# The gather pipeline of a mixture-of-experts layer given out in another order, with 92 instead of 96 gathered tokens

## Chip, cores and metric

The kernel runs on one core of a Trainium2 chip. The metric is the device time of one launch in microseconds (us); the time before is the median of three runs. "Profile" and "trace" mean one execution recorded by the hardware profiler. PE is the matrix engine (TensorE), DVE is VectorE, ACT is ScalarE, POOL is GpSimd and SP is the sync engine, which here only issues loads.

## The reference, cut to what matters

Two blocks run over 256 tokens of width 2048. The first (gated convolution and attention) and the front of the second (convolution and a state-space branch) are not touched by the change. What matters is the last layer, a product-key expert layer with 16384 experts of one neuron each, in float32:

```python
s = einsum('thcd,hcnd->thcn', (xb @ w_q), sub_keys)   # 8 heads, 2 halves, 128 keys
s_top, i_top = top_k(s, 16)
cand = s_top[:, :, 0, :, None] + s_top[:, :, 1, None, :]
best, pos = top_k(cand, 16)                            # 16 experts a head, 128 a token
gates = softmax(best)
act = gelu(einsum('td,thkd->thk', xb, u_tab[expert]))
y = einsum('thk,thkd->td', gates * act, v_tab[expert])
x = x + y;  return rmsnorm(x, norm_final)
```

## The kernel before

The first 1226 us of the trace are dense layers. Then the 256 tokens of the expert layer are split by token and computed in two ways at the same time.

**Dense, for the last NT = 160 tokens.** All 16384 experts are computed, 128 at a time. A *u step* multiplies one 1 MB tile of `u` with the normed tokens (16 matrix products, recorded as 32 matmuls of 160 columns, since each float32 product takes two) and ACT writes gelu of the result (`u_step`). A *v step* multiplies one 1 MB tile of `v` with the weighed activations and adds into PSUM (`v_step`). There are 128 of each: 60 u steps first, then v and u alternating (68 pairs), then 60 v steps. The last `LAST` v steps are done bank by bank, so that one bank is finished while the next is multiplied. Tiles come through a ring of `NR = 5` buffers on SP's queue; the load of tile n+5 goes out when step n has used its buffer. PE writes u results to two PSUM banks in turn, so it can be at most two u steps ahead of ACT.

The weights of the dense part are the gates spread into a 128x128 table for each token. `gbuild` makes them from one-hot rows: four tokens at a time, DVE and ACT write the rows, PE multiplies them (8 matmuls), ACT copies the result out, and every 16 tokens a DMA writes the table `gd` to memory. `gload` reads a block of it back for 8 experts' rows, and DVE's `weigh` multiplies the activations with it ahead of each v step.

**Gathered, for the first NS_ = 96 tokens.** `sparse` fetches only the 128 chosen rows of a token: in each of 3 groups of 32 tokens, one gather brings 128 rows of 8 KB (32 tokens x 4 experts), 1 MB, into one of 5 buffers. An *item* is one gather and one DVE instruction of 2.3 us on it: a product and sum with the token (u item) or a scaled add (v item). The 192 items come as four u items, then four v items of the block of u items before. After four u items ACT takes gelu of their 4 columns. The gather of item m+5 is issued on POOL right behind item m, whose buffer it needs. At the end the four partial sums of a token go through memory (`sd`) and are added on DVE, normed and written out.

**The order.** There is no scheduler: instructions stand on each engine in the order in which the Python code runs. After each step, `Weave.run(budget)` lets generators (`topk`, `sparse`) emit as much as a budget of estimated ns allows; a `yield None` ends a generator's turn until the next step. `run_fine` does the same for `gbuild`, four times in a step. Each engine works through its own list, so an instruction that waits holds up all behind it on that engine. `hand_out` puts expert indices and gates of the first 128 tokens into the layout that the gathers read (`rbuf`).

Of the kernel before, what the change touches and what calls it, by code (L numbers as in the profile page):

```python
# [107 lines left out]
def body(ctx, tc, xT, par, wst, kst, bblk, cblk, gfin, uexp, vexp, out):  # L108
# [1090 lines left out]
    flat = lambda ap: ap.rearrange("p h k -> p (h k)")  # L1199
    sp_ready = [False]  # L1200

    def hand_out():


        V = nc.vector
        V.scalar_tensor_tensor(out=flat(ab[:, 0]), in0=flat(idx[:, 0]), scalar=float(P), in1=flat(idx[:, 1]),
                               op0=ALU.mult, op1=ALU.add)
        V.tensor_copy(flat(abu[:, 0]), flat(ab[:, 0]))
        V.tensor_copy(abr[:, P:2 * P], flat(gat))
        both = abr.rearrange("p (c s) -> p c s", c=2)  # L1210
        for g in range(SG):
            for q in range(4):
                nc.gpsimd.dma_start(
                    rbuf[32 * q:32 * q + 32, 64 * g:64 * g + 64].rearrange("p (c s) -> p c s", c=2),
                    both[32 * g:32 * g + 32, :, 32 * q:32 * q + 32])
        sp_ready[0] = True

    def topk():
        V = nc.vector
        for tt in range(2):  # L1220
            for h in range(NH + 1):
# [29 lines left out]
            yield 2500
            o4 = scor[tt].rearrange("p (h a b) -> p h a b", h=8, a=16)
            for c in range(2):
                for h in range(0, NH, 4):
                    for q in range(4):
                        V.tensor_tensor(out=o4[:, h + q], in0=ab[:, c, h + q, :, None].to_broadcast([P, 16, 16]),
                                        in1=iota[:, None, 0:16].to_broadcast([P, 16, 16]), op=ALU.is_equal)
                    for q in range(4):
                        V.tensor_tensor(out=o4[:, h + q], in0=o4[:, h + q],
                                        in1=ixf[:, h + q, c, None, :].to_broadcast([P, 16, 16]), op=ALU.mult)  # L1260
                    V.tensor_reduce(out=idx[:, c, h:h + 4, :], in_=o4[:, h:h + 4], axis=AX.X, op=ALU.add)
                    yield 3900
# [15 lines left out]
    GB = [B[6], B[7]]  # L1278
    oh = [[S[22][:, (8 * n + k) * P:(8 * n + k + 1) * P] for k in range(8)] for n in range(2)]
    pend_g = []  # L1280

    def gbuild():
        for t4 in range(NT // 4):
            sg = stg[(t4 // 4) % 2].rearrange("p (i t) -> p t i", t=16)
            pb = GB[t4 % 2]
            t = NS_ + t4 * 4
            nc.vector.tensor_tensor(
                out=S[22][:, (t % 8) * P:(t % 8 + 4) * P].rearrange("p (t j) -> p t j", t=4),
                in0=iota[:, None, :].to_broadcast([P, 4, P]),
                in1=i2T[:, t:t + 4, None].to_broadcast([P, 4, P]), op=ALU.is_equal)  # L1290
            for q in range(4):
                o, tq = oh[1][(t + q) % 8], slice(t + q, t + q + 1)
                if q < 1:
                    nc.scalar.activation(o, iota, AF.Abs, scale=-1.0, bias=i1T[:, tq])
                    nc.scalar.activation(o, o, AF.Relu, scale=ngT[:, tq], bias=gT[:, tq])
                else:
                    nc.vector.tensor_scalar(o, iota, i1T[:, tq], gT[:, tq], op0=ALU.is_equal, op1=ALU.mult)
            yield 1650 - 256 * 1
            pend_g.append((t4, pb, sg))
            if len(pend_g) > 1:  # L1300
                gmm(*pend_g.pop(0))
        while pend_g:
            gmm(*pend_g.pop(0))
            yield 500

    def gmm(t4, pb, sg):
        for q in range(4):
# [4 lines left out]
        if t4 % 4 == 3:  # L1312
            nc.scalar.dma_start(gd[t4 // 4], stg[(t4 // 4) % 2].rearrange("p (i t) -> p i t", t=16))

    gblk = lambda b: stg[b % 2][:, 0:8 * NT].rearrange("p (n i t) -> p n i t", n=NT // 16, i=8)

    def gload(b):
        nc.gpsimd.dma_start(gblk(b), gd[:, :, 8 * b:8 * b + 8, :].rearrange("n p i t -> p n i t"))

    def weigh(i):  # L1320

        a3 = act_at(i).rearrange("p (n t) -> p n t", n=NT // 16)
        nc.vector.tensor_tensor(out=a3, in0=a3, in1=gblk(i // 8)[:, :, i % 8, :], op=ALU.mult)  # L1323
        if i % 8 == 7 and i // 8 + 2 < 16:
            gload(i // 8 + 2)


    acc_s, x_rep, gaddr = S[10], S[19], rbuf.bitcast(U32)
    dots = sqsum

    def sparse():
# [4 lines left out]
        flat_b = [(g, n) for g in range(SG) for n in range(8)]  # L1336
# [5 lines left out]
        items += [("v", SG - 1, 28 + k) for k in range(4)]  # L1342

        def gather(m):
            kind, g, k = items[m]
            nc.gpsimd.indirect_dma_start(  # L1346
                out=gb[m % len(gb)][:], out_offset=None, in_=uexp if kind == "u" else vexp,
                in_offset=bass.IndirectOffsetOnAxis(ap=gaddr[:, 64 * g + k:64 * g + k + 1], axis=0))

        def rows(g):  # L1350
            for q in range(4):
                nc.gpsimd.dma_start(x_rep[32 * q:32 * q + 32, :], S[18][32 * g:32 * g + 32, :])

        rows(0)
        for m in range(len(gb)):
            gather(m)
        yield None
        for m, (kind, g, k) in enumerate(items):
            buf = gb[m % len(gb)]
            d, a = dots[:, 32 * g + k:32 * g + k + 1], dots[:, P + 32 * g + k:P + 32 * g + k + 1]  # L1360
            if kind == "u":
                V.tensor_tensor_reduce(out=buf, in0=buf, in1=x_rep, scale=1.0, scalar=0.0,  # L1362
                                       op0=ALU.mult, op1=ALU.add, accum_out=d)
# [282 lines left out]
```

## Time and profile before

| what | value |
|---|---|
| median of 3 runs | 2569.36 us (2566.88 to 2573.03) |
| profiled execution, its own time | 2564.76 us |
| its span in the trace | 2563.0 us |
| PE busy | 2397.4 us, 94% |
| DVE, ACT, POOL busy | 62%, 27%, 26% |
| moved by DMA | 741.94 MB |

The span runs from the first instruction to the last. Busy time of PE is modelled, so its share is no measure of how near it is to its peak; what counts is which wait ends last in each stretch. The DMA share is that of the core's 16 DMA engines (1.01 is all of them all the time).

### The profile page before, as it was taken

The page shows a single profiled execution, that of the slowest core. Times are in us where ns is not written, and L with a number is a line of the kernel's source. Part 1 is how long each engine was busy: PE and PEld are TensorE (multiplying, and loading weights), DVE is VectorE, ACT ScalarE, POOL GpSimd, SP SyncE. Part 2 cuts the span into 40 slices and gives each one's busy share as a digit, 9 for nine tenths or more (in the row PEclk, how much of TensorE's full clock was granted, in tenths as well). Part 3 has the DMA queues.
Part 4 walks back from the last instruction along what each step waited for, and adds up shares of the span by engine and source line. Part 5 has one row for each costly group of instructions (what it writes and reads, how often), then busy time and mean ns, then how long its engine had stood idle before and what let it go on. Part 6 is the DMA issues. An engine that isn't in the chain of part 4 may idle for free.

```text
span 2563.0 us, 40064 instructions
## 1 busy us (share of the span) xinstructions
PE 2397.4 (94%) x16832; PEld 2270.2 (89%) x16832; DVE 1587.9 (62%) x2379; ACT 696.5 (27%) x1043; POOL 659.5 (26%) x853
## 2 busy tenths in 40 slices
PE   8999999999999999999879994999999899999987
PEld 7888888899999999888879994988888888999887
DVE  6767777589999977567497665344444344414433
ACT  5544454443244445453114520000000000000002
POOL 1887888300000000230202124221111221021100
PEclk9999999999999999999989997999999999999999
DMA  6455556565555444564789999999999999999994
GB/s 234 175 187 188 191 181 215 196 239 206 197 205 183 173 174 176 192 226 165 251 309 389 393 396 360 379 416 421 417 416 416 381 418 416 394 355 412 412 351 176
DMA packets 110004, 741.94 MB, mean 289 GB/s; under 512 B 12832, under 2 KB 13184, under 8 KB 24032
## 3 DMA queue, kind: packets, MB, share of 16 engines
q1 hardware_dynamic: 65760, 474.50, 49.1%
q0 software_dynamic: 36864, 241.81, 23.7%
q10 hardware_dynamic: 7200, 23.07, 2.4%
q8 instruction: 132, 2.16, 0.3%
q14 instruction: 48, 0.39, 0.0%
HBM read 707.00 MB, written 29.10 MB: 287 GB/s over the span
## 4 chain that ended last, share of the span: by engine, by line
PE 63%; DMA 27%; DVE 5%; issue 2%; ACT 1%; POOL 1%; SPq 0%; POOLq 0%; DVEq 0%; ACTq 0%
DMA s<-in_vexp_dram 14%; PE b L270 13%; PE b L1475 10%; PE b L1458 10%; DMA s<-in_wst_dram 9%; PE b L271 7%; PE b L255 4%; PE b L257 4%; PE b L256 4%; PE b L400 2%; DVE s L173 2%; PE b L248 2%; PE b L247 2%; PE b L246 2%; DMA s<-in_uexp_dram,rbuf 2%
## 5 line engine op out<-in xcount | busy, mean ns | idle before, releaser
L1458 PE MATMUL b<-s,s 128*128 128x160 f32 x4096 | 584.9, 302 | 61.3 <-ACT s L1461 38.5
L1475 PE MATMUL b<-s,s 128*128 128x160 f32 x4096 | 583.4, 302 | 54.5 <-DMA s<-in_vexp_dram 44.5
L1458 PEld LDWEIGHTS b<-s,s 128*128 128x128 f32 x4096 | 565.5, 191 | 73.3 <-ACT s L1461 39.2
L1475 PEld LDWEIGHTS b<-s,s 128*128 128x128 f32 x4096 | 563.7, 191 | 71.9 <-issue 57.6
L270 PE MATMUL b<-s,s 128*128 128x512 f32 x1680 | 597.6, 399 | 0.0
L271 PE MATMUL b<-s,s 128*128 128x256 f32 x1680 | 471.5, 281 | 9.1 <-DVE s L173 9.0
L173 DVE TENSOR_TENSOR s<-s,s 128x2048 fp32r<-128x2048 f32 x192 | 452.4, 2358 | 28.1 <-issue 12.3
L1362 DVE CUSTOM_DVE_ANT_0 s<-s,s 128x2048 f32<-128x2048 f32 x96 | 219.7, 2291 | 275.0 <-DMA s<-in_uexp_dram,rbuf 241.6
L270 PEld LDWEIGHTS b<-s,s 128*128 128x128 f32 x1680 | 315.9, 188 | 71.4
L1374 DVE SCALAR_TENSOR_TENSOR s<-s,sqsum,s 128x2048 f32<-128x2048 f32 x93 | 218.7, 2351 | 258.8 <-DMA s<-in_vexp_dram,rbuf 258.1
L167 ACT ACTIVATE s<-s 128x2048 fp32r<-128x2048 f32 x192 | 365.7, 1906 | 9.6 <-DMA s<-in_wst_dram 9.6
L271 PEld LDWEIGHTS b<-s,s 128*128 128x128 f32 x1680 | 317.7, 189 | 13.4 <-DVE s L173 12.6
L255 PE MATMUL b<-s,s 128*128 128x256 f32 x896 | 256.6, 286 | 0.0
L257 PE MATMUL b<-s,s 128*128 128x256 f32 x896 | 253.5, 283 | 0.0
L256 PE MATMUL b<-s,s 128*128 128x256 f32 x896 | 253.5, 283 | 0.0
L1461 ACT ACTIVATE s<-b 128x160 f32<-128x160 f32 x128 | 38.0, 300 | 765.3 <-PE b L1458 756.1
L1346 POOL DMA_INDIRECT s<-in_vexp_dram,rbuf x96 | 106.6, 1110 | 458.8 <-DVE sqsum L1362 196.1
L1346 POOL DMA_INDIRECT s<-in_uexp_dram,rbuf x96 | 114.3, 1191 | 382.3 <-DVE s L1323 174.7
L255 PEld LDWEIGHTS b<-s,s 128*128 128x128 f32 x896 | 171.8, 192 | 3.7 <-issue 2.9
L256 PEld LDWEIGHTS b<-s,s 128*128 128x128 f32 x896 | 171.9, 192 | 0.3
L257 PEld LDWEIGHTS b<-s,s 128*128 128x128 f32 x896 | 171.9, 192 | 0.0
L814 POOL TENSOR_TENSOR sqsum<-sqsum,s 128x256 f32<-128x256 f32 x28 | 57.9, 2067 | 385.5 <-ACT s L812 385.5
(302 smaller groups left out, 2441.8 us busy)
## 6 DMA issues: line engine op xcount, KB each, us to landing
s<-in_wst_dram SPq DMA_DIRECT2D x320, 1024.0 KB
s<-in_vexp_dram SPq DMA_DIRECT2D x128, 1024.0 KB
gd<-s ACTq DMA_DIRECT2D x10, 1024.0 KB
s<-gd POOLq DMA_DIRECT2D x16, 640.0 KB
tabd<-s POOLq DMA_DIRECT2D x32, 256.0 KB
s<-tabd ACTq DMA_DIRECT2D x32, 256.0 KB
xd<-s POOLq DMA_DIRECT2D x4, 1024.0 KB
s<-in_bblk_dram ACTq DMA_DIRECT2D x8, 512.0 KB
```

The costliest lines, as they stand in the source:

```text
L167: nc.scalar.activation(hi_of(i), raw_of(i), AF.Copy)
L173: nc.vector.tensor_tensor(out=lo_of(i), in0=raw_of(i), in1=FV(hi_of(i)), op=ALU.subtract)
L255: nc.tensor.matmul(ps, a, xh, start=(j == 0), stop=False)
L256: nc.tensor.matmul(ps, a, xl, start=False, stop=False)
L257: nc.tensor.matmul(ps, b, xh, start=False, stop=(j == len(perm) - 1))
L270: nc.tensor.matmul(ps, a, x2, start=(j == 0), stop=False)
L271: nc.tensor.matmul(ps[:, :T], b, x2[:, :T], start=False, stop=(j == len(perm) - 1))
L1346: nc.gpsimd.indirect_dma_start(out=gb[m % len(gb)][:], out_offset=None, in_=uexp if kind == "u" else vexp, in_offset=bass.IndirectOffsetOn ...
L1362: V.tensor_tensor_reduce(out=buf, in0=buf, in1=x_rep, scale=1.0, scalar=0.0, op0=ALU.mult, op1=ALU.add, accum_out=d)
L1374: V.scalar_tensor_tensor(out=acc_s, in0=buf, scalar=a, in1=acc_s, op0=ALU.mult, op1=ALU.add)
L1458: nc.tensor.matmul(ps, raw[:, k * P:(k + 1) * P], nv(k)[:, NS_:T], start=(k == 0), stop=(k == KT - 1))
L1475: nc.tensor.matmul(acc[d], raw[:, d * P:(d + 1) * P], act_at(i), start=False, stop=(i == P - 1 and (d % 3 == 2 or d == KT - 1)))
```

## The change

1. Tokens: the third group has 28 instead of 32 tokens, so 92 tokens are gathered and 164 are dense. Every dense matmul has 164 columns. The 64 gathers of the third group fetch 112 rows, not 128. `weigh` gets a second small instruction for the 4 tokens beyond 160, whose table stays on the chip (`rest`). Loads and stores of all gathered tokens (`sd`, `xrow`, `out`) have 92 rows.
2. `hand_out` is split: the indices go out before the softmax of the gates, and the index work of the first four heads (`picks`) moves up into the top-k loop.
3. `sparse` issues its first five gathers and then lets `AHEAD = 5` turns go by before the first item. The gelu of four u items is emitted two items later.
4. The first two `gload`s are issued on ACT's queue, not POOL's.
5. Budgets: while `gbuild` runs, `sparse` gets 1000 instead of 1500 for a step and `gbuild` 3400 instead of 2700. `LAST` is 2, not 4.

```diff
-SG = 3
-NS_ = 32 * SG
+GROUPS = [(0, 32), (32, 32), (64, 28)]
+NS_ = 92
...
-    def hand_out():
+    def hand_out(c):
...
+                if h == 5:
+                    yield from picks(tt, 0)
+            yield from picks(tt, 4)
+            if tt == 0:
+                hand_out(0)
             V.tensor_tensor(out=gat, in0=best, in1=best[:, :, 0:1].to_broadcast([P, 8, 16]), op=ALU.subtract)
             nc.scalar.activation(gat, gat, AF.Exp)
...
             if tt == 0:
-                hand_out()
+                hand_out(1)
...
+        if GR:
+            nc.vector.tensor_tensor(out=a[:, GT:NT], in0=a[:, GT:NT], in1=rest[:, i, :], op=ALU.mult)
...
+            if m == 0:
+                rows(0)
+        for _ in range(AHEAD):
+            yield None
+        late = []
...
                 if k % 4 == 3:
-                    lo, hi = 32 * g + k - 3, 32 * g + k + 1
-                    nc.scalar.activation(dots[:, P + lo:P + hi], dots[:, lo:hi], AF.Gelu_apprx_tanh)
+                    late.append((m + 2, acts[:, k - 3:k + 1], dots_[:, k - 3:k + 1]))
...
+            while late and m >= late[0][0]:
+                _, dst, src = late.pop(0)
+                nc.scalar.activation(dst, src, AF.Gelu_apprx_tanh)
...
-        u_step(i, 1500.0 if weave.fine else 4200.0, 2700.0 / 4)
+        u_step(i, 1000.0 if weave.fine else 4200.0, 3400.0 / 4)
...
-    gload(0)
-    gload(1)
+    gload(0, nc.scalar)
+    gload(1, nc.scalar)
...
-    LAST = 4
+    LAST = 2
```

**First place: ACT, where the first gelu of the gathered part stands.** L1461 (L1488 after) is the gelu that empties a u step's PSUM bank (`b0` or `b1`), L1366 (L1401 after) the gelu of four gathered columns in `sqsum`. Before, it stands behind the 9th u step's row:

```order
L1461 ACTIVATE s14_10958<-b1_66 128x160
L1461 ACTIVATE s14_10958<-b0_65 128x160
L1271 ACTIVATE s24_86<-b5_70 128x128 x3
L1272 ACTIVATE s24_86<-b5_70 128x128
L1366 ACTIVATE sqsum_88<-sqsum_88 128x4
L1461 ACTIVATE s14_10958<-b1_66 128x160
```

In the changed program the first one stands behind the 29th u step's row, among the copies of `gbuild` (L1323, L1307, L1308):

```order
L1326 DMA gd_10086<-s11_10074 128x2048
L1307 ACTIVATE s22_10081<-iota_10171,s24_86 128x128
L1308 ACTIVATE s22_10081<-s22_10081,s24_86 128x128
L1401 ACTIVATE sqsum_88<-sqsum_88 128x4
L1488 ACTIVATE s16_10966<-b1_66 128x164
```

It moved back by 20 u steps. Before, the first seven stand behind u steps 9, 24, 33, 45, 51, 56 and 60; after, behind 29, 38, 46, 50, 55, 59 and 64. The copies of `gbuild` stand behind u steps 28 to 47 before and 26 to 42 after.

**Second place: POOL, where the u steps end and the v steps begin.** L1346 (L1364 after) are gathers, L1318 the `gload`s, and the memset is what PE's first matmuls into the v sums need. Before:

```order
L1346 DMA s13_11202<-in_vexp_dram,rbuf_87 128x2048
L1346 DMA s5_11198<-in_vexp_dram,rbuf_87 128x2048
L1318 DMA s23_10082<-gd_10086 128x10x128
L1318 DMA s11_10074<-gd_10086 128x10x128
L1468 MEMSET s22_12892 128x512
L1346 DMA s6_11199<-in_vexp_dram,rbuf_87 128x2048
```

After, on POOL:

```order
L1364 DMA s5_11196<-in_uexp_dram,rbuf_87 128x2048
L1364 DMA s6_11197<-in_uexp_dram,rbuf_87 128x2048
L1495 MEMSET s22_12915 128x512
L1364 DMA s7_11198<-in_uexp_dram,rbuf_87 128x2048
L1364 DMA s12_11199<-in_vexp_dram,rbuf_87 128x2048
```

and on ACT, where the two loads went:

```order
L1488 ACTIVATE s8_12645<-b1_66 128x164
L1488 ACTIVATE s8_12645<-b0_65 128x164
L1401 ACTIVATE sqsum_88<-sqsum_88 128x4
L1331 DMA s23_10082<-gd_10086 128x10x128
L1331 DMA s11_10074<-gd_10086 128x10x128
L1488 ACTIVATE s8_12645<-b1_66 128x164
```

The two loads left POOL's list and stand on ACT behind the gelu of item 40. Ahead of this place 51 gathers stand on POOL before, 47 after, and 46 items on DVE before, 42 after. When `gbuild` ends, 24 items stand ahead on DVE before (47 u steps done), 11 after (42 done). Ahead of the loads of the saved tokens (L1510, L1537 after) 161 gathers stand before, 157 after; the last item stands with step 240 of 256 before, 246 after.

**Third place: PE's last steps.** L1475 (L1502 after) are v products into banks `b2` to `b7`, L1553 (L1580 after) the transposes of a finished bank; `s0` to `s4` are the tile buffers. Before, four tiles are taken bank by bank:

```order
L1475 MATMUL b3_68<-s8_12626,s2_80 128x160 x3
L1475 MATMUL b3_68<-s8_12626,s3_10964 128x160 x3
L1475 MATMUL b3_68<-s8_12626,s4_10965 128x160 x3
L1475 MATMUL b3_68<-s8_12626,s0_78 128x160 x3
L1553 MATMUL b0_65<-ident_74,s14_16747 128x128 x3
```

After, two:

```order
L1502 MATMUL b3_68<-s8_12645,s4_10971 128x164 x3
L1502 MATMUL b3_68<-s8_12645,s0_78 128x164 x3
L1580 MATMUL b0_65<-ident_74,s14_16938 128x128 x3
```

Half of the products that stood between two banks' transposes moved ahead of the first bank.

## Rows read from the trace of the kernel before

**Rows 1.** Windows: stretch, length, busy us (x records) by engine, PEclk, DMA share, GB/s.

```profile
1367.00:1491.00 124.00, 124.00 (x969) 124.00 (x968) 88.55 (x185) 73.47 (x141) 15.77 (x14) 1.00 0.99 396
1491.00:1575.00 84.00, 59.55 (x411) 58.82 (x409) 51.03 (x34) 5.89 (x17) 31.24 (x22) 0.88 1.01 416
1575.00:1597.00 22.00, 8.95 (x34) 8.27 (x35) 6.79 (x10) 0.20 (x1) 6.27 (x6) 0.52 0.71 267
1597.00:2206.00 609.00, 559.46 (x3943) 538.05 (x3943) 264.74 (x240) 19.93 (x74) 135.91 (x133) 1.00 1.01 409
2206.00:2259.00 53.00, 51.47 (x373) 50.62 (x373) 13.13 (x16) 1.61 (x6) 0.31 (x2) 1.00 0.84 330
2259.00:2344.00 85.00, 84.62 (x622) 84.21 (x621) 29.04 (x30) 0.60 (x3) 21.20 (x23) 1.00 1.01 405
2344.00:2457.00 113.00, 104.82 (x736) 100.42 (x736) 49.92 (x53) 1.90 (x4) 17.69 (x19) 1.00 1.01 412
2457.00:2531.00 74.00, 66.24 (x466) 65.14 (x467) 17.92 (x26) 4.21 (x4) 5.08 (x10) 0.98 0.93 314
```

**Rows 2.** Waits from 1220 to 1600 us: waiter, releaser, us in total, times, longest.

```profile
ACT sqsum L1366 <- DVE sqsum L1362: 95.5, 7, 27.8
...
PE b L1458 <- ACT s L1461: 38.5, 3, 20.3
```

**Rows 3.** The chain that ended last: start, length, what.

```profile
1225.84 4.36 PE b L1458 x32
...
1575.42 14.73 DMA s<-gd
...
1814.48 20.10 DMA s<-in_vexp_dram
...
2523.25 7.63 DMA s<-in_vexp_dram
```

**Rows 4.** Timeline of PE: start, length, instruction, [idle before <-releaser].

```profile
1372.45 1.05 PE L1309 MATMUL b<-s 128*128 128x128 f32 x8
1373.34 2.34 PE L1458 MATMUL b<-s,s 128*128 128x160 f32 x16
1375.52 1.05 PE L1309 MATMUL b<-s 128*128 128x128 f32 x8
```

**Rows 5.** Timeline of POOL, same columns.

```profile
1577.41 0.61 POOL L1468 MEMSET s<- 128x512 f32 x1
...
2205.21 0.95 POOL L1346 DMA_INDIRECT s<-in_vexp_dram,rbuf  x1 [4.04 <-DVE s L1323]
2258.84 0.94 POOL L1510 DMA_DIRECT2D s<-xd  x1 [52.69 <-PE b L1458]
```

**Rows 6.** Timeline of DVE, same columns.

```profile
1244.07 1.22 DVE L1261 TENSOR_REDUCE s<-s 128x64 f32<-128x1024 f32 x1
...
1248.00 1.22 DVE L1261 TENSOR_REDUCE s<-s 128x64 f32<-128x1024 f32 x1
...
1545.31 2.29 DVE L1362 CUSTOM_DVE_ANT_0 s<-s,s 128x2048 f32<-128x2048 f32 x1 [2.68 <-DMA s<-in_uexp_dram,rbuf]
...
1550.29 2.29 DVE L1362 CUSTOM_DVE_ANT_0 s<-s,s 128x2048 f32<-128x2048 f32 x1 [2.68 <-DMA s<-in_uexp_dram,rbuf]
...
2457.37 2.35 DVE L1374 SCALAR_TENSOR_TENSOR s<-s,sqsum,s 128x2048 f32<-128x2048 f32 x1 [2.50 <-DMA s<-in_vexp_dram,rbuf]
...
2483.70 2.29 DVE L1391 TENSOR_TENSOR s<-s,s 96x2048 f32<-96x2048 f32 x1 [22.57 <-DMA s<-sd]
...
2500.56 2.29 DVE L1391 TENSOR_TENSOR s<-s,s 96x2048 f32<-96x2048 f32 x1 [3.00 <-DMA s<-xrow]
...
2532.11 0.66 DVE L1546 TENSOR_TENSOR s<-b,s 128x480 f32<-128x480 f32 x1 [22.72 <-PE b L1475]
...
2549.14 0.64 DVE L1546 TENSOR_TENSOR s<-b,s 128x480 f32<-128x480 f32 x1
...
2552.10 0.30 DVE L1546 TENSOR_TENSOR s<-b,s 128x160 f32<-128x160 f32 x1
```

More of the change, by code (lines that the diff above doesn't have):

```diff
@@ L1110, in body @@
     gd = drp.tile([NT // 16, P, P, 16], F32, name="gd")
+    GT, GR = NT // 16 * 16, NT % 16
     for c in range(2):
@@ L1200, in body @@
     sp_ready = [False]
-    def hand_out():
+    def hand_out(c):
         V = nc.vector
[L1206 to L1211, printed above, removed]
-            for q in range(4):
[L1213 to L1216, printed above, removed]
+        if c == 0:
+            V.scalar_tensor_tensor(out=flat(ab[:, 0]), in0=flat(idx[:, 0]), scalar=float(P), in1=flat(idx[:, 1]),
+                                   op0=ALU.mult, op1=ALU.add)
+            V.tensor_copy(flat(abu[:, 0]), flat(ab[:, 0]))
+        else:
+            V.tensor_copy(abr[:, P:2 * P], flat(gat))
+        for g, (t0, n) in enumerate(GROUPS):
+            for q in range(4):
+                nc.gpsimd.dma_start(rbuf[n * q:n * q + n, 64 * g + 32 * c:64 * g + 32 * c + 32],
+                                    abr[t0:t0 + n, P * c + 32 * q:P * c + 32 * q + 32])
+        if c == 0:
+            sp_ready[0] = True
@@ new lines, in picks @@
+    def picks(tt, h):
+        V = nc.vector
+        hs = slice(h, h + 4)
+        V.tensor_copy(ixf[:, hs], ix[:, hs])
+        V.tensor_scalar(abu[:, 0, hs], pos[:, hs], 4, None, op0=ALU.logical_shift_right)
+        V.tensor_scalar(abu[:, 1, hs], pos[:, hs], 15, None, op0=ALU.bitwise_and)
+        V.tensor_copy(ab[:, :, hs], abu[:, :, hs])
+        yield 900
+        o4 = scor[tt].rearrange("p (h a b) -> p h a b", h=8, a=16)
+        for c in range(2):
+            for q in range(4):
+                V.tensor_tensor(out=o4[:, h + q], in0=ab[:, c, h + q, :, None].to_broadcast([P, 16, 16]),
+                                in1=iota[:, None, 0:16].to_broadcast([P, 16, 16]), op=ALU.is_equal)
+            for q in range(4):
+                V.tensor_tensor(out=o4[:, h + q], in0=o4[:, h + q],
+                                in1=ixf[:, h + q, c, None, :].to_broadcast([P, 16, 16]), op=ALU.mult)
+            V.tensor_reduce(out=idx[:, c, hs, :], in_=o4[:, hs], axis=AX.X, op=ALU.add)
+            yield 3900
@@ L1250, in topk @@
             V.tensor_tensor(out=gat, in0=gat, in1=gsum[:, 8:16, None].to_broadcast([P, 8, 16]), op=ALU.mult)
[L1251 to L1262, printed above, removed]
             if tt == 0:
-                hand_out()
+                hand_out(1)
             yield None
@@ L1280, in body @@
     pend_g = []
+    rest = S[24][:, 0:P * GR].rearrange("p (i t) -> p i t", t=GR) if GR else None
     def gbuild():
         for t4 in range(NT // 4):
-            sg = stg[(t4 // 4) % 2].rearrange("p (i t) -> p t i", t=16)
+            sg = stg[(t4 // 4) % 2].rearrange("p (i t) -> p t i", t=16) if t4 * 4 < GT else rest.rearrange("p i t -> p t i")
             pb = GB[t4 % 2]
@@ L1311, in gmm, with gload @@
                              pb.rearrange("p (t i) -> p t i", t=4), AF.Copy)
-        if t4 % 4 == 3:
+        if t4 % 4 == 3 and t4 * 4 < GT:
             nc.scalar.dma_start(gd[t4 // 4], stg[(t4 // 4) % 2].rearrange("p (i t) -> p i t", t=16))
-    gblk = lambda b: stg[b % 2][:, 0:8 * NT].rearrange("p (n i t) -> p n i t", n=NT // 16, i=8)
-    def gload(b):
-        nc.gpsimd.dma_start(gblk(b), gd[:, :, 8 * b:8 * b + 8, :].rearrange("n p i t -> p n i t"))
+    gblk = lambda b: stg[b % 2][:, 0:8 * GT].rearrange("p (n i t) -> p n i t", n=GT // 16, i=8)
+    def gload(b, eng):
+        eng.dma_start(gblk(b), gd[:, :, 8 * b:8 * b + 8, :].rearrange("n p i t -> p n i t"))
     def weigh(i):
-        a3 = act_at(i).rearrange("p (n t) -> p n t", n=NT // 16)
+        a = act_at(i)
+        a3 = a[:, 0:GT].rearrange("p (n t) -> p n t", n=GT // 16)
         nc.vector.tensor_tensor(out=a3, in0=a3, in1=gblk(i // 8)[:, :, i % 8, :], op=ALU.mult)
+        if GR:
+            nc.vector.tensor_tensor(out=a[:, GT:NT], in0=a[:, GT:NT], in1=rest[:, i, :], op=ALU.mult)
         if i % 8 == 7 and i // 8 + 2 < 16:
-            gload(i // 8 + 2)
+            gload(i // 8 + 2, nc.gpsimd)
     acc_s, x_rep, gaddr = S[10], S[19], rbuf.bitcast(U32)
+    AHEAD = 5
     dots = sqsum
@@ L1335, in sparse @@
         gb = slots([5, 6, 7, 12, 13])
-        flat_b = [(g, n) for g in range(SG) for n in range(8)]
+        flat_b = [(g, n) for g in range(len(GROUPS)) for n in range(8)]
         items = []
@@ L1341, in sparse @@
                 items += [("v", flat_b[j - 1][0], 4 * flat_b[j - 1][1] + k) for k in range(4)]
-        items += [("v", SG - 1, 28 + k) for k in range(4)]
+        items += [("v", len(GROUPS) - 1, 28 + k) for k in range(4)]
         def gather(m):
             kind, g, k = items[m]
+            n = 4 * GROUPS[g][1]
             nc.gpsimd.indirect_dma_start(
-                out=gb[m % len(gb)][:], out_offset=None, in_=uexp if kind == "u" else vexp,
-                in_offset=bass.IndirectOffsetOnAxis(ap=gaddr[:, 64 * g + k:64 * g + k + 1], axis=0))
+                out=gb[m % len(gb)][0:n, :], out_offset=None, in_=uexp if kind == "u" else vexp,
+                in_offset=bass.IndirectOffsetOnAxis(ap=gaddr[0:n, 64 * g + k:64 * g + k + 1], axis=0))
@@ L1350, in rows @@
         def rows(g):
+            t0, n = GROUPS[g]
             for q in range(4):
-                nc.gpsimd.dma_start(x_rep[32 * q:32 * q + 32, :], S[18][32 * g:32 * g + 32, :])
-        rows(0)
+                nc.gpsimd.dma_start(x_rep[n * q:n * q + n, :], S[18][t0:t0 + n, :])
         for m in range(len(gb)):
             gather(m)
-        yield None
+            if m == 0:
[3 more added lines that the diff above has]
+        late = []
         for m, (kind, g, k) in enumerate(items):
-            buf = gb[m % len(gb)]
-            d, a = dots[:, 32 * g + k:32 * g + k + 1], dots[:, P + 32 * g + k:P + 32 * g + k + 1]
+            t0, n = GROUPS[g]
+            buf = gb[m % len(gb)][0:4 * n, :]
+            dots_, acts = dots[0:4 * n, 32 * g:32 * g + 32], dots[0:4 * n, P + 32 * g:P + 32 * g + 32]
+            ac = acc_s[0:4 * n, :]
@@ L1361, in sparse @@
             if kind == "u":
-                V.tensor_tensor_reduce(out=buf, in0=buf, in1=x_rep, scale=1.0, scalar=0.0,
-                                       op0=ALU.mult, op1=ALU.add, accum_out=d)
+                V.tensor_tensor_reduce(out=buf, in0=buf, in1=x_rep[0:4 * n, :], scale=1.0, scalar=0.0,
+                                       op0=ALU.mult, op1=ALU.add, accum_out=dots_[:, k:k + 1])
                 if k % 4 == 3:
-                    lo, hi = 32 * g + k - 3, 32 * g + k + 1
-                    nc.scalar.activation(dots[:, P + lo:P + hi], dots[:, lo:hi], AF.Gelu_apprx_tanh)
+                    late.append((m + 2, acts[:, k - 3:k + 1], dots_[:, k - 3:k + 1]))
@@ L1367, in sparse @@
             else:
+                a = acts[:, k:k + 1]
                 if k % 4 == 0:
-                    a4 = dots[:, P + 32 * g + k:P + 32 * g + k + 4]
-                    V.tensor_tensor(out=a4, in0=a4, in1=rbuf[:, 64 * g + 32 + k:64 * g + 36 + k], op=ALU.mult)
+                    a4 = acts[:, k:k + 4]
+                    V.tensor_tensor(out=a4, in0=a4, in1=rbuf[0:4 * n, 64 * g + 32 + k:64 * g + 36 + k], op=ALU.mult)
                 if k == 0:
-                    V.tensor_scalar(acc_s, buf, a, None, op0=ALU.mult)
+                    V.tensor_scalar(ac, buf, a, None, op0=ALU.mult)
@@ L1373, in sparse @@
                 else:
-                    V.scalar_tensor_tensor(out=acc_s, in0=buf, scalar=a, in1=acc_s, op0=ALU.mult, op1=ALU.add)
+                    V.scalar_tensor_tensor(out=ac, in0=buf, scalar=a, in1=ac, op0=ALU.mult, op1=ALU.add)
+            while late and m >= late[0][0]:
+                _, dst, src = late.pop(0)
+                nc.scalar.activation(dst, src, AF.Gelu_apprx_tanh)
             if m + len(gb) < len(items):
                 gather(m + len(gb))
-            if kind == "u" and k == 31 and g < SG - 1:
+            if kind == "u" and k == 31 and g < len(GROUPS) - 1:
```

7 lines of the change are left out of this document (2 added, 5 removed).

## Prediction

> **What bounds the kernel now.** I read the windows first, then the waits, then the chain and the timelines. The expert layer's start to its end is 1337 of 2563 us, and the change touches nothing ahead of it but a little DVE work. In it two things take turns as the bound. While `gbuild` runs and just after (1367 to 1575) the 16 DMA engines are busy all the time; PE is too until 1491, but then falls to 59.55 of 84 us [rows 1]. From 1597 to 2206 the DMA share is 1.01 and PE is busy 559 of 609 us: 3943 matmul records, at 32 a step, are 123 steps, 4.94 us each, while a step of PE alone takes 4.36 [rows 1, 3]. So DMA sets the pace there, with one 1 MB tile a step and the gathers beside it. In three stretches DMA isn't the bound: at 1575 to 1597 it moves 267 GB/s instead of 416, since all wait for the first gate tables; at 2206 to 2259 PE is busy 51.47 of 53 us; and in the first 19 steps after that PE is busy 84.62 of 85 [rows 1]. The second has its cause on POOL: the load of the saved tokens waits 52.69 us for the last u step, and the gathers stand behind it [rows 5].
>
> The waits show what is visible to mend ahead of 1600: ACT stood 95.5 us in the gathered gelu, so PE waited 38.5 us for a PSUM bank that ACT had not emptied [rows 2]. But a wait of PE is only worth its time if DMA isn't needed for the same stretch; that is the point on which the sum turns.
>
> **The change, part by part.** *Start of the v steps.* Before, DVE could weigh at 1575.42 + 14.73 = 1590.2 [rows 3]. After: a u step is 4.36 x 164/160 = 4.47 us; a `gbuild` block costs PE 3.07 (from 1372.45 to 1375.52) less half a step of 2.18, so 0.89 [rows 4]. The first gelu now stands 20 u steps later, so nothing I see stops PE until `gbuild` ends at step 42: 1225.8 + 42 x 4.47 + 41 x 0.89 = 1450. But only 11 items stand ahead of it, and with the four gathers that fit behind them 15 have landed. The `gload`s stand behind the gelu of item 40, so 25 more gathers and the 18 tiles of steps 43 to 60 must land: 43 transfers. At 416 GB/s [rows 1] 1.05 MB takes 2.52 us, together 108 us, so 1558; with one DVE item and the gate table's load (nothing to 14.73, I take 10, since it is no longer behind gathers in POOL's list) the v steps start at 1571. That is **-19.6 us**. The bounds: if a gather takes the 4.98 us from item to item that DVE shows when tiles come too [rows 6], 25 of them end at 1575 and v starts at 1587 (-3.6); with a table load of nothing and 2.4 us a transfer, -34.
>
> *What is left to move then.* Before, 51 gathers were in, 141 left. After, 40, and 4 more during the table's load: 148 left, less 64 x 1/8 for the 112-row gathers, so 140 in full ones. One transfer less: **-2.5**. If a 112-row gather takes as long as a full one, this is +17.5 instead.
>
> *The hole at 1575 to 1597.* (416 - 267)/416 x 22 = 7.9 us of DMA time was lost [rows 1]. After, gathers are still under way when v starts: **-7** (bounds: -7.9, 0).
>
> *Wider matmuls.* +0.11 us a step. Where DMA sets the pace (4.94) it is hidden under the 0.5 us that PE waits in each step. Where PE does (2206 to 2259, the 19 steps behind it and the 14 from 2457 on; 373, 622 and 466 records [rows 1]) it isn't: 45 x 0.11 = **+5**. If the cover is gone everywhere from the first v step on, 196 x 0.11 = +21.5.
>
> *LAST.* From the last tile's load (2523.25) to the end are 39.75 us [rows 3]. After, three whole steps (13.4) and a sixth-by-sixth rest of two (0.28 x 6 = 1.7) end the first bank 15.1 us later. Then come the banks: before, 2532.11 to 2552.10, 20 us for five, paced by PE; after, PE has half the products and the pace is that of the last bank before, 2552.10 - 2549.14 = 2.96 [rows 6], so 14.8. 15.1 + 30.9 - 5.2 = 40.8: **+1**. It would gain up to 8.7 (two steps) if the last tile's arrival, 7.63 us after its issue, set the end; with three steps behind the issue it doesn't.
>
> *At nothing.* The earlier hand-out: the halves of `hand_out` both stand on POOL ahead of the first gather, and the first item waits for turn 25 anyway. The moved `picks` are DVE pieces of 1248.00 - 1244.07 = 3.93 us [rows 6], two in a half, in a stretch where PE's matmuls of the last residual steps need DVE; uncovered they cost 8 us, but the same pieces leave the chain behind. 128 small multiplications in `weigh`: DVE is busy 264.74 of 609 us there [rows 1]. The two table loads hold ACT, where u step 60's gelu stands behind them, but v can't start without them either. The memset that PE needs still stands behind gathers on POOL (1577.41 before [rows 5]), at a like time as the tables.
>
> *Rows of 92 and 28.* The four loads of the partial sums and the one of x end the sparse work: first needed at 2483.70, the last at 2500.56, 5.6 us apart, with the last item at 2457.37 [rows 6]; the last piece comes 41 us after it. After, they end near 2500 while the first bank is ready only near 2514, so 14 us of lateness are hidden. [...] No run here shows a load of 92 rows. [...]
>
> **Sum.** -19.6 - 2.5 - 7 + 5 + 1 = -23. The span goes from 2563.0 to 2540, the profiled execution's own time from 2564.76 to about 2542. The median of the runs shown is 4.6 above that execution, so about **2546**; its own range is 2533 to 2560. About 0.2% (5 us) is what a measurement of this kernel can tell from no change.
>
> **Rivals.** *The gathers are the end's bound, and PE keeps up* (0.18). All transfers to the last item: 8 fewer gathers, but 6 more tiles, since the last item stands with step 246 instead of 240: -2, 5 us. With the hole filled (-7) the last item ends at 2459.7 - 12 = 2447. If PE is then at step 245, only the sparse chain is left: 43 us to its last add, 6 to its norm, then the banks, 25.7: 2522, so a median of 2529. For it: PE has 0.5 us of slack in every step. Against it: tiles were five ahead of PE then as well, and PE stood at step 238, two behind (466 records to 2531 [rows 1] are 14.6 steps, and at 2531 some 252.6 of 256 were done).
>
> *The start gives little* (0.13). Gathers at 4.98 us each: -3.6 - 2.5 - 7 + 5 + 1 = -7, a median of 2562, at the edge of no change. For it: DVE's pace of 4.98 in a stretch where PE was waiting too. Against: that pace was half the DMA engines' work, tiles had the rest, and tiles stop when PE stops.
>
> *PE's width is paid in every step* (0.07), slower. Chain: a tile's load starts when its buffer is free and takes 20.10 us [rows 3]; if that is latency and not a queue, a round of five is 20.1 plus one step, every step costs +0.11 (+21.5), and fewer bytes give nothing: -19.6 + 17.5 + 21.5 + 1 = +20, a median of 2590. It decides once PE's own step exceeds the pace that DMA gives, 4.94. Against: a share of 1.01 is a queue.
>
> *The loads of 92 rows are late* (0.05), slower. [...]
>
> **How the numbers follow.** The sum has 0.57. Faster by over 0.2%: 0.57 + 0.18 + a part (0.03) of the second rival = 0.78; same 0.10, the rest of that; slower 0.12, the last two. The range, 2518 to 2568, takes in the first rival with its spread and the second, and leaves out the two slow ones and the ends.
>
> **What would show it.** ACT's wait in the gathered gelu falls from 95.5 to under 40 us before v, and comes just ahead of v, with PE idle there; no PE wait for ACT before 1500; the DMA share from 1360 to 1450 well under 0.99; the first v matmul near 1571; steps near 4.94 until some 2185 and the 53 us behind the saved tokens' load still there, ending near 2240; the last item near 2450, with PE at step 241 or so. Wrong: a v start after 1585, a step of 5.05 in the saturated stretch, or a last add later than the first bank.

## The result

The changed kernel takes 2752.89 us (median of 4 runs, 2752.1 to 2757.18), the kernel before 2568.12 (2565.16 to 2573.03) beside it: a ratio of 1.0721, 95% interval 1.07 to 1.0742. It is 7.2% slower; 2546 us and a gain were forecast, and the range ended at 2568.

Up to some 2020 us the two kernels run almost alike: from 1600 to 2000 us both move 411 GB/s. Then the third group of gathered tokens begins, the one with 28 tokens; its first 112-row gather is issued at 2013.38, and the rate of the transfers falls while the DMA engines stay busy. The windows of the changed kernel show it (columns as in [rows 1]):

```profile
1367.00:1453.00 86.00, 86.00 (x671) 86.00 (x670) 58.89 (x136) 58.17 (x110) 6.70 (x6) 1.00 0.87 320
1453.00:1568.00 115.00, 81.66 (x554) 80.91 (x553) 65.91 (x47) 7.31 (x22) 39.84 (x28) 0.85 1.01 416
...
1900.00:2000.00 100.00, 93.33 (x641) 89.24 (x640) 47.58 (x55) 3.26 (x12) 19.98 (x21) 1.00 1.01 416
2000.00:2100.00 100.00, 80.42 (x515) 77.89 (x515) 35.47 (x40) 2.65 (x10) 25.14 (x20) 0.93 1.02 327
2100.00:2200.00 100.00, 74.95 (x433) 72.32 (x433) 29.01 (x35) 1.94 (x7) 20.38 (x17) 0.86 1.02 269
2200.00:2300.00 100.00, 71.78 (x444) 69.15 (x443) 20.38 (x25) 2.24 (x8) 12.10 (x8) 0.91 1.02 266
2300.00:2400.00 100.00, 90.07 (x632) 89.19 (x630) 26.24 (x38) 1.93 (x8) 13.69 (x15) 0.98 0.90 276
2400.00:2500.00 100.00, 69.83 (x422) 67.21 (x423) 33.05 (x51) 0.21 (x1) 13.60 (x14) 0.91 1.02 264
2500.00:2600.00 100.00, 67.65 (x411) 64.77 (x410) 30.17 (x48) 1.90 (x4) 13.43 (x14) 0.91 1.02 257
2600.00:2700.00 100.00, 81.63 (x512) 79.69 (x513) 30.45 (x44) 1.12 (x1) 6.73 (x11) 0.90 1.01 285
2700.00:2751.00 51.00, 36.22 (x258) 34.31 (x256) 15.93 (x41) 12.20 (x32) 0.51 (x1) 0.88 0.33 127
```

One of the same windows in the kernel before:

```profile
2100.00:2200.00 100.00, 92.10 (x649) 88.28 (x648) 44.58 (x39) 3.22 (x12) 17.10 (x18) 1.00 1.01 418
```

The last two columns are what the reader is to see: a share of 1.02 at 269 and 266 GB/s, where the stretch before 2000 had 1.01 at 416 and the kernel before has 1.01 at 418. So a busy share says that the engines have work in hand, not how fast it moves. As an estimate from these rows, with all 16 busy a row of 8 KB holds an engine for 16 x 8192 B / 416 GB/s = 0.315 us in the first case and 0.493 at 266 GB/s. The work is not more: from 2000 us to the end these windows move 201 MB in 752 us, while before moved 207 MB from there on in 563. The difference of 189 us is the whole difference of the two traced executions (2751.6 and 2563.0 us); by the medians the loss is 185.

The tile loads pay as well as the gathers. In the chain that ended last, a tile of `v` landed 20.10 us after its buffer was free [rows 3]; in the changed kernel, at the place where the third group begins and behind it (`wst` holds the tiles of `u`):

```profile
1979.34 20.12 DMA s<-in_vexp_dram
...
2034.69 35.72 DMA s<-in_wst_dram
2070.54 7.62 PE b L1485 x32
2087.10 28.04 DMA s<-in_vexp_dram
```

PE, which had waited some 0.5 us in a step, now waits for its tiles: from 2040 us on 126.6 us in all for those of `v` and 25.0 for those of `u`. Its granted clock, 1.00 from 1900 to 2000, is 0.86 on average from 2100 to 2200. Behind the wait for the tile of `u` above it is 0.50 in windows of 1 us from 2070 to 2076 and 0.74 from 2076 to 2077, so in some 6 of the step's 7.62 us. I read that as a consequence and not the cause: PE is idle for 25 of those 100 us, and with full gathers (e2 below) the clock there is 1.00. DVE's items show the gathers' own pace, 7 us where [rows 6] had 4.98:

```profile
2059.80 2.29 DVE L1386 CUSTOM_DVE_ANT_0 s<-s,s 112x2048 f32<-112x2048 f32 x1 [4.76 <-DMA s<-in_uexp_dram,rbuf]
...
2066.72 2.29 DVE L1386 CUSTOM_DVE_ANT_0 s<-s,s 112x2048 f32<-112x2048 f32 x1 [4.30 <-DMA s<-in_uexp_dram,rbuf]
```

Ahead of the v steps the change did part of what was forecast. The waits from 1220 to 1610 us, which answer to [rows 2]:

```profile
ACT sqsum L1401 <- DVE sqsum L1386: 54.1, 3, 20.3
...
PE b L1485 <- ACT s L1488: 20.3, 2, 12.2
...
DVE s L1337 <- DMA s<-gd: 12.3, 1, 12.3
```

and the first product of the v steps on PE, in the kernel before:

```profile
1590.55 7.24 PE L1475 MATMUL b<-s,s 128*128 128x160 f32 x32 [9.97 <-DVE s L1323]
```

and in the changed one:

```profile
1586.21 7.46 PE L1502 MATMUL b<-s,s 128*128 128x164 f32 x32 [7.54 <-DVE s L1339]
```

### The profile page after: what moved, and what is told of

Read it like the earlier page. It is cut to its first block, busy times and chain, and to the rows that moved or that the text cites. A ratio compares the mean times of both kernels' runs of the same rounds, so it can differ in the third digit from the quotient of the medians.

```text
span 2751.6 us, 40234 instructions
## 1 busy us (share of the span) xinstructions
PE 2474.7 (90%) x16840; PEld 2346.4 (85%) x16840; DVE 1599.1 (58%) x2519; ACT 699.0 (25%) x1046; POOL 678.6 (25%) x863
## 4 chain that ended last, share of the span: by engine, by line
PE 60%; DMA 33%; DVE 5%; ACT 1%; issue 1%; POOL 0%; SPq 0%; DVEq 0%; ACTq 0%; POOLq 0%
DMA s<-in_vexp_dram 19%; PE b L270 12%; PE b L1485 11%; DMA s<-in_wst_dram 10%; PE b L1502 9%; PE b L271 6%; PE b L255 4%; PE b L257 4%; PE b L256 4%; DMA s<-in_vexp_dram,rbuf 2%; DVE s L173 2%; PE b L248 2%; PE b L247 2%; PE b L246 2%; PE b L400 2%; PE b L1322 1%
## 5 line engine op out<-in xcount | busy, mean ns | idle before, releaser
L1502 PE MATMUL b<-s,s 128*128 128x164 f32 x4096 | 644.2, 320 | 154.2 <-DMA s<-in_vexp_dram 141.4
L1502 PEld LDWEIGHTS b<-s,s 128*128 128x128 f32 x4096 | 622.6, 203 | 172.7 <-issue 127.9
L1485 PE MATMUL b<-s,s 128*128 128x164 f32 x4096 | 603.4, 307 | 58.9 <-DMA s<-in_wst_dram 38.6
L1485 PEld LDWEIGHTS b<-s,s 128*128 128x128 f32 x4096 | 583.7, 193 | 70.0 <-issue 49.1
L173 DVE TENSOR_TENSOR s<-s,s 128x2048 fp32r<-128x2048 f32 x192 | 452.6, 2359 | 26.8 <-issue 12.3
L1386 DVE CUSTOM_DVE_ANT_0 s<-s,s 128x2048 f32<-128x2048 f32 (+1 forms) x96 | 219.5, 2292 | 367.6 <-DMA s<-in_uexp_dram,rbuf 338.0
L270 PEld LDWEIGHTS b<-s,s 128*128 128x128 f32 x1680 | 315.8, 188 | 71.2
L1398 DVE SCALAR_TENSOR_TENSOR s<-s,sqsum,s 128x2048 f32<-128x2048 f32 (+1 forms) x93 | 218.7, 2352 | 241.3 <-DMA s<-in_vexp_dram,rbuf 240.3
L271 PEld LDWEIGHTS b<-s,s 128*128 128x128 f32 x1680 | 317.7, 189 | 12.9 <-DVE s L173 12.2
L1488 ACT ACTIVATE s<-b 128x164 f32<-128x164 f32 x128 | 38.7, 304 | 897.8 <-PE b L1485 878.8
L1364 POOL DMA_INDIRECT s<-in_uexp_dram,rbuf x96 | 127.6, 1330 | 530.6 <-DVE s L1398 253.4
L1364 POOL DMA_INDIRECT s<-in_vexp_dram,rbuf x96 | 109.8, 1144 | 464.9 <-DVE sqsum L1386 317.1
L255 PEld LDWEIGHTS b<-s,s 128*128 128x128 f32 x896 | 171.8, 192 | 3.7 <-issue 2.9
L256 PEld LDWEIGHTS b<-s,s 128*128 128x128 f32 x896 | 171.9, 192 | 0.3
L257 PEld LDWEIGHTS b<-s,s 128*128 128x128 f32 x896 | 171.9, 192 | 0.0
```

Of the source, the lines that this page charges most:

```text
L173: nc.vector.tensor_tensor(out=lo_of(i), in0=raw_of(i), in1=FV(hi_of(i)), op=ALU.subtract)
L255: nc.tensor.matmul(ps, a, xh, start=(j == 0), stop=False)
L256: nc.tensor.matmul(ps, a, xl, start=False, stop=False)
L257: nc.tensor.matmul(ps, b, xh, start=False, stop=(j == len(perm) - 1))
L270: nc.tensor.matmul(ps, a, x2, start=(j == 0), stop=False)
L271: nc.tensor.matmul(ps[:, :T], b, x2[:, :T], start=False, stop=(j == len(perm) - 1))
```

## The experiments

The theory (A): gathers of 112 rows keep all transfers slow as long as they run. The main rival (B): the new order costs the time.

| kernel | median us | ratio to before, 95% interval |
|---|---|---|
| e1: change with 96 tokens | 2560.14 | 0.9974 (0.9964 to 0.9983) |
| e2: change, 92 tokens, gathers filled up to 128 rows | 2569.64 | 1.0006 (0.9997 to 1.0015) |
| e3: before with 92 tokens | 2763.53 | 1.075 (1.0729 to 1.077) |
| e4: change with 88 tokens, 96-row gathers | 2717.51 | 1.0598 (1.0573 to 1.0622) |
| e6: e1, gelu at once | 2560.73 | 0.9979 (0.997 to 0.9988) |
| e7: e1, LAST = 4 | 2564.39 | 0.9993 (0.9984 to 1.0002) |
| e8: e1, table loads on POOL | 2561.17 | 0.9979 (0.9968 to 0.9989) |
| e10: before, LAST = 2 | 2568.32 | 1.0014 (1.0005 to 1.0023) |
| e11: e1, LAST = 1 | 2561.39 | 0.9984 (0.9975 to 0.9993) |
| e12: e1, last loads of 128 rows | 2552.42 | 0.9946 (0.9934 to 0.9958) |

**The order without the 28 tokens (e1).**

```diff
-GROUPS = [(0, 32), (32, 32), (64, 28)]
-NS_ = 92
+GROUPS = [(0, 32), (32, 32), (64, 32)]
+NS_ = 96
```

> The changed kernel with its third group back at 32 tokens (96 gathered tokens, 160 columns), everything else of the change kept. Theory A (the 112-row gathers of the third group slow every transfer from 2043 us on): the fall to 265 GB/s goes away, the pitch of the items after 2040 us is again about 5 us, the time is 2545 to 2570 us, at or a little below before's 2568. Rival B (the new order of the work costs the time, by the later gelus, the five steps of lead or LAST = 2): 2700 us or more, with the same slow third group. Rival C (both in part): 2600 to 2700 us.

2560.14 us: the whole loss is gone, and what is left of the change is a small gain. Rivals B and C fall.

**92 tokens, full gathers (e2).**

```diff
+            if n < 32 and c == 0:
+                nc.gpsimd.dma_start(rbuf[4 * n:P, 64 * g:64 * g + 32], abr[0:P - 4 * n, 0:32])
...
-            n = 4 * GROUPS[g][1]
+            n = P
             nc.gpsimd.indirect_dma_start(
```

> The changed kernel with 92 tokens and 164 columns as it is, but each gather of the third group fetches 128 rows: the 16 rows behind the 112 are fetched for nothing, with indices copied from other tokens, and nothing reads them. Theory A: more bytes are moved (64 x 16 rows of 8 KB, 8.4 MB) and yet the kernel is about 190 us faster than the changed one, 2550 to 2580 us. Rival D (the slow part is the 164 columns, the remainder that is weighed apart, or the vectors of 112 partitions): 2740 us or more. If a partial gather were only priced by its bytes, these rows would cost 8.4 MB at 417 GB/s, 20 us, on top of 2753.

2569.64 us. Everything of the change is there but the row count of the gathers, and fetching 16 useless rows in each of 64 gathers makes it 183 us faster (before took 2567.48 beside it and 2568.12 beside the changed kernel). The window of e2 that answers to the changed kernel's 269 GB/s:

```profile
2100.00:2200.00 100.00, 95.52 (x659) 91.73 (x657) 43.34 (x51) 3.26 (x12) 25.38 (x20) 1.00 1.01 418
```

So neither the 164 columns nor the second small multiplication makes the loss; they are part of the 9.5 us that e2 takes more than e1. PE's granted clock is 1.00 in this window, where the changed kernel had 0.86. A 112-row gather costs 183 / 64 = 2.9 us more than a full one, the delay of the tiles beside it included.

**92 tokens in before's order (e3).** The edit is the token part of the change alone, put into the kernel before.

```diff
-SG = 3
-NS_ = 32 * SG
+GROUPS = [(0, 32), (32, 32), (64, 28)]
+NS_ = 92
...
```

> The kernel before with 92 gathered tokens alone: groups of 32, 32 and 28 tokens, 112-row gathers in the third, 164 columns, its own order of work. Theory A: slower than before by about what the change was slower, 2740 to 2780 us, with 260 to 280 GB/s in the third group. Rival E (112 rows are slow only together with the new order, such as the table reloads on another queue or the gathers further ahead): 2560 to 2600 us.

2763.53 us, and 264 GB/s from 2100 to 2200. The slow part needs nothing of the new order.

**Another partial count (e4).**

```diff
-GROUPS = [(0, 32), (32, 32), (64, 28)]
-NS_ = 92
+GROUPS = [(0, 32), (32, 32), (64, 24)]
+NS_ = 88
```

> [...] Theory A1 (a gather is slow when its rows do not split over the engines as 128 do, whatever the count): again 260 to 290 GB/s after 2040 us; 64 x 16 rows fewer than the changed kernel are 8.4 MB, at 265 GB/s 32 us, so 2710 to 2740 us. [...]

2717.51 us, with 256 to 286 GB/s in the stretches of 100 us from 2100 to 2500: 96 rows are as bad, and 112 is no special case. How the rows split over the engines, which A1 takes for the reason, no run shows. The gain over the changed kernel, 35 us, is about the 32 of the fewer bytes at the slow rate.

**The transfers by themselves (e5, e9).** The first probe:

> A kernel that computes nothing of the reference: it only moves rows of 8 KB, 24 transfers in each of twelve stretches, five in flight: gathers of 128, 120, 112, 96 and 64 rows from partition 0 and of 64 rows to partitions 32 to 95; the same number of plain loads of 128, 112, 64 and 64 (32 to 95) rows; then gathers of 128, and of 112, beside full tile loads. [...] Rival Q (it is the gather's own queue that is slow with a part of the rows): plain loads of 112 and 64 rows stay at 400 GB/s or more per full engine time, gathers alone fall. Rival R (the rate falls with the rows that are missing): 112 rows 365, 96 rows 310, 64 rows 210 GB/s wherever they go.

It gave little: its plain loads were not held back to their own stretches and ran beside the gathers. Only its first stretch can be read, 128 rows beside 128 rows at 422 GB/s.

The second has a sum over all buffers between the stretches, and 20 transfers in each.

```diff
         for n, b in enumerate(gb + tb):
             V.tensor_copy(scr[:, n:n + 1], b[:, 0:1])
+        V.tensor_reduce(out=scr[:, 10:11], in_=scr[:, 0:10], axis=AX.X, op=ALU.add)
         for b in gb + tb:
-            V.memset(b[:, 0:1], 0.0)
+            V.tensor_copy(b[:, 0:1], scr[:, 10:11])
...
-    N = 24
+    N = 20
```

> The transfers of the probe of rows again, 20 in each of the twelve stretches, now with a sum over one column of all ten buffers between the stretches, so that none of one stretch starts before the last of the stretch ahead has landed: gathers of 128, 120, 112, 96, 64 rows from partition 0 and of 64 rows to partitions 32 to 95; plain loads of 128, 112, 64, 64 (32 to 95) rows; gathers of 128, and of 112, beside full tile loads. It computes nothing of the reference. [...] Rival Q (the gather's queue): plain loads of 112 rows at 400 GB/s. Rival R (in proportion to the rows): 365 GB/s for 112, 310 for 96, 210 for 64 at either place.

Its windows, one inside each stretch in the order of the expectation (stretch, length, busy us of DVE and POOL, clock, DMA share, GB/s):

```profile
20.00:50.00 30.00, 2.30 (x8) 10.33 (x11) 1.00 1.01 423
75.00:140.00 65.00, 0.31 (x2) 12.65 (x13) 1.00 1.02 229
165.00:215.00 50.00, 0.31 (x2) 11.04 (x12) 1.00 1.02 259
235.00:285.00 50.00, 0.46 (x3) 11.79 (x13) 1.00 1.01 250
300.00:340.00 40.00, 0.46 (x3) 11.63 (x13) 1.00 1.02 208
350.00:370.00 20.00, 0.15 (x1) 13.39 (x16) 1.00 0.99 401
385.00:420.00 35.00, 0.15 (x1) 0.00 (x0) 1.00 1.01 423
440.00:485.00 45.00, 0.31 (x2) 0.00 (x0) 1.00 1.02 305
505.00:540.00 35.00, 0.31 (x2) 0.00 (x0) 1.00 1.02 206
552.00:572.00 20.00, 0.15 (x1) 0.00 (x0) 1.00 1.00 406
590.00:665.00 75.00, 0.26 (x2) 13.10 (x14) 1.00 1.01 422
695.00:800.00 105.00, 0.77 (x5) 12.82 (x14) 1.00 1.01 293
```

Gathers of 128, 120, 112, 96 and 64 rows from partition 0 move 423, 229, 259, 250 and 208 GB/s, so the rate does not follow the count (rival R falls). Plain loads of 112 and 64 rows are slow too, 305 and 206, so it isn't the gather's queue (rival Q falls). The same 64 rows at partitions 32 to 95 go at 401 and 406: for them the place in SBUF decides. And 112-row gathers and full tile loads beside them move 293 together, where with 128-row ones it is 422. All that at a share of 0.99 to 1.02, so it is not that fewer of the 16 engines had work.

The rates also say where the 2.9 us of e2 went. Alone, a 112-row gather takes 3.54 us at 259 GB/s and a full one 2.48 us at 423 (estimates from these rows). That is 1.06 us more, so by these rates more than half of the 2.9 went to the transfers beside it. The kernel's 264 to 276 GB/s from 2100 to 2500 lie below the probe's 293; why stays open.

Why the place counts as it does (401 against 208 GB/s for 64 gathered rows, 1.93 times), and why 120, 112 and 96 rows from partition 0 move only 229 to 259, no run shows: the trace does not say which engine moved which row.

**The parts of the order (e6, e7, e8, e10, e11).** All but e10 change one thing in e1:

```diff
-                    late.append((m + 2, acts[:, k - 3:k + 1], dots_[:, k - 3:k + 1]))
+                    late.append((m, acts[:, k - 3:k + 1], dots_[:, k - 3:k + 1]))
```

> The 96-token version of the changed kernel with the gathered items' gelu given out right behind its fourth dot product again, as before, the rest of the change kept. If the later gelu is what it gains (the prediction's 20 us for the start of the v steps): 2570 to 2580 us, with single waits of ScalarE for VectorE above 25 us between 1220 and 1600. If the stretch from 1367 to 1600 is bound by the transfers, of which neither version has fewer: 2557 to 2564 us, the same as with the later gelu (2560).

```diff
-    LAST = 2
+    LAST = 4
```

> The 96-token version of the changed kernel with LAST = 4 in place of 2, four steps behind the gathers' end instead of two. The prediction put LAST at 1 us: 2559 to 2562 us. If the steps behind the last gathers fill VectorE's tail of sums, two more of them at 4.9 us each could be worth up to 10 us either way: 2550 or 2570 us.

```diff
-    gload(0, nc.scalar)
-    gload(1, nc.scalar)
+    gload(0, nc.gpsimd)
+    gload(1, nc.gpsimd)
```

> The 96-token version of the changed kernel with the first two loads of the weight table issued by GpSimd again. The prediction gave ScalarE's queue 7 us, a hole in the transfers between 1575 and 1597 us that it would close; in the run with 96 tokens the window 1550 to 1600 moved 335 GB/s against 347 of before, so the hole is still there. If the queue makes no difference: 2557 to 2563 us. If it does what was predicted: 2565 to 2570 us.

e10 is before with `LAST = 2`:

```diff
-    LAST = 4
+    LAST = 2
```

> The kernel before with LAST = 2 in place of 4, nothing else changed. With 96 tokens the changed kernel took 2564.4 us with LAST = 4 and 2560.1 with 2. If LAST alone is worth those 4 us: 2560 to 2564 us here, ratio 0.998 to 0.999. If the prediction's price holds (1 us the other way) and the difference lies in the rest of the order: 2566 to 2570 us.

and e11 is e1 once more:

```diff
-    LAST = 2
+    LAST = 1
```

> The 96-token version of the changed kernel with LAST = 1. If each step taken out of LAST is worth 2 us, as from 4 to 2: 2557 to 2560 us. If the end is bound by VectorE's tail of sums, which takes the kept-back steps as cover, 2560 to 2566 us.

The gelu's delay by two items and ACT's queue are worth nothing that can be measured (2560.73 and 2561.17 against 2560.14). e6 undoes only that delay: its first gathered gelu runs at 1336.41 us, that of e1 at 1365.82, that of before at 1294.76. The rest of the shift comes from the five turns of lead and the budgets, which no run undoes by themselves, and none undoes the split of `hand_out`. `LAST` from 4 to 2 gains 3 to 4 us in the new order (e7 against e6, e8 and e1) and costs 3.4 in the old one (2568.32 against 2564.94 beside it); 1 gives no more. Which part of the order `LAST` works together with stays open.

**A use of it (e12).** In e1, DVE's last sums come from five loads of 96 rows, and PE's last v steps run beside them. Windows and PE's timeline of e1:

```profile
2440.00:2475.00 35.00, 32.62 (x232) 31.35 (x231) 16.06 (x16) 0.00 (x0) 1.99 (x2) 1.00 1.02 413
...
2490.00:2515.00 25.00, 18.48 (x135) 18.05 (x134) 6.61 (x5) 0.00 (x0) 0.00 (x0) 1.00 1.01 256
```

```profile
2505.86 4.58 PE L1502 MATMUL b<-s,s 128*128 128x160 f32 x32 [3.08 <-DMA s<-in_vexp_dram]
2513.89 18.21 PE L1502 MATMUL b<-s,s 128*128 128x160 f32 x120 [3.45 <-DMA s<-in_vexp_dram]
```

The last two tiles come late. The edit puts the four partial sums and x behind one another in memory, so that each load can take 128 rows:

```diff
-    xrow = drp.tile([NS_, D], F32, name="xrow")
-    sd = drp.tile([4, NS_, D], F32, name="sd")
+    sd = drp.tile([4 * NS_ + P, D], F32, name="sd")
...
-    nc.gpsimd.dma_start(xrow, S[19][0:NS_, :])
+    nc.gpsimd.dma_start(sd[4 * NS_:4 * NS_ + P, :], S[19])
...
-        for q in range(4):
-            nc.gpsimd.dma_start(parts[q], sd[q])
-        nc.gpsimd.dma_start(parts[4], xrow)
+        for q in range(5):
+            nc.gpsimd.dma_start(gb[q], sd[q * NS_:q * NS_ + P, :])
```

> The 96-token version of the changed kernel, in which the five loads that bring back the partial sums and x near 2480 us take 128 rows instead of 96 (32 rows of the neighbouring part come along and nothing reads them). In the run with 96 tokens the window 2490 to 2515 moved 256 GB/s at a share of 1.01, and PE waited 3.08 and 3.45 us there for its last tiles. Theory P (loads of a part of the rows hold up the tile loads beside them): the window moves about 400 GB/s, although 1.3 MB more are fetched, those two waits of PE go and the time falls by 3 to 6.5 us, to 2554 to 2557 us, a ratio of 0.995 to 0.996. Rival (the waits are the last tiles' own lateness, whatever runs beside them): 2558 to 2563 us, ratio 0.997 to 0.998, as with 96 rows; the added bytes alone would cost 3 us.

2552.42 us, ratio 0.9946 (0.9934 to 0.9958): faster than both kernels and than e1, by a little more than the 3 to 6.5 us expected. Its window and timeline:

```profile
2490.00:2515.00 25.00, 25.00 (x187) 25.00 (x186) 7.34 (x5) 0.00 (x0) 1.57 (x3) 1.00 1.01 420
```

```profile
2474.71 51.31 PE L1500 MATMUL b<-s,s 128*128 128x160 f32 x376 [0.37 <-DMA s<-in_vexp_dram]
```

256 GB/s became 420 with more bytes to fetch, and PE runs through to its first finished bank.

## Why the prediction was wrong

**The step that failed** is *What is left to move then*: "148 left, less 64 x 1/8 for the 112-row gathers, so 140 in full ones". It priced a partial gather by its bytes, and its other bound, "as long as a full one" (+17.5), assumed that the worst is to save nothing. Measured, the 64 gathers cost 183 us more than full ones (changed kernel against e2): 112 rows move more slowly than 128, and the transfers beside them are held up too (293 against 422 GB/s in e9). No rival had that mechanism; the fourth had the loads of 92 rows late, but neither the 64 gathers nor the tiles beside them. A hint was in [rows 6]: before's loads of 96 rows, 0.79 MB, came 5.6 us apart, while gathers of 1.05 MB came 4.98 apart with tiles beside them; I took the 5.6 as given and did not ask why. The bound was read rightly, and that is why the slip weighed so much: DMA set the pace, so slower transfers went straight to the end.

**Start of the v steps** (-19.6, bounds -3.6 and -34): -4.3 here, -8.2 in e1 (1582.31). `gbuild` ended as worked out near 1450, and the 43 transfers went at the 416 GB/s assumed; the 2.4 us a transfer in the bound of -34 no run shows: at the 423 GB/s of e9 a full one takes 2.48 (an estimate). But from 1453 to 1568 there were 47.8 MB to move, 45.6 full transfers instead of 43, so that the gelu of item 40 came at 1568.4 where some 1561 had been counted; and the first product stood 17.8 us behind it, where 10 were put down for the table's load. The gelu's place was meant as the reason. Of its shift e6 takes back the two items, and the first product stays where it was (1582.33 against 1582.31 in e1); an account that fits is that the share of 0.87 from 1367 to 1453, where before had 0.99 in [rows 1], is DMA time not used, and the same bytes are moved later.

**The hole at 1575 to 1597** (-7): not closed. These 22 us move 221 GB/s, before 267. DVE stood 12.3 us in front of its first weighing, waiting for the table, with items behind it; POOL's next gather waited 13.25 us for one of them, so none was issued from 1575 to 1589. The queue makes no difference (237 GB/s in e8, 239 in e1).

**Wider matmuls** (+5, up to +21.5): e2 against e1 is +9.5, which holds these columns and the other small parts of 92 tokens.

**LAST** (+1): -3 to -4 in the new order, +3.4 in the old; mis-sized either way.

**Rows of 92** (no term): no run shows the lateness that has 0.05 among the rivals. The loads are 5 to 7 us apart in the changed kernel (the sums at 2678.92, 2684.48, 2691.41 and 2696.56), where the 96 rows of [rows 6] had 5.6, so the fourth rival falls. The prediction went from 96 rows to 92 and did not ask what full loads would bring: e12 gains 7 to 8 us over e1 by them.

In a row the runs give 2567.5 - 7.3 (order, e1) + 9.5 (rest of the 92 tokens, e2) + 183 (row count). This ends at the measured time by construction, since each term is the difference of two neighbouring runs; what it shows is their sizes. The forecast of -23 had the order at more than it gave and the row count at next to nothing.

**What would show it.** ACT's wait fell to 54.1, not under 40; PE's first wait for ACT began at 1494, where none was expected before 1500; the first v product came after 1585, named as a sign of error; the share of 1367 to 1453 was well under 0.99, as said. In the saturated stretch a step stayed near 4.94 only until the third group began.

## What to carry to other kernels

A transfer to part of the partitions is not priced by its bytes: look at the rate beside the busy share in the stretch, since here a share of 1.01 or 1.02 stood beside 423 GB/s and beside 206 alike. Before a row count of 128 is cut, try to fetch the missing rows for nothing; here that gave back 183 us, and the same edit on five late loads gained 7 to 8 more. Where half of the rows are enough, their place counts: 64 rows at partitions 32 to 95 moved nearly twice as fast as at 0 to 63 (401 and 406 GB/s against 208 and 206).

## What the hardware showed that was not expected

None of this was in the prediction. 64 rows at partitions 32 to 95 moved 401 GB/s as gathers and 406 as plain loads, the same at 0 to 63 208 and 206. 120 rows (229 GB/s) were slower than 112 (259), though nearer to 128 (423). Plain loads of 112 rows were faster (305) than gathers of 112 (259). Why stays open for all three.
